# A two-layer encoder in float32: the opening on unscaled tokens, and memory's heads later in layer A

## The chip, the cores and the metric

The kernel runs on one core of one Trainium2 chip, as one program. The metric is the device time in microseconds (us) of one execution; lower is better. The engines have these names: PE is the matrix engine, with its weight loads listed apart as PEld; DVE the vector engine; ACT the scalar (activation) engine; POOL is GpSimd; SP and ACT issue the DMAs here.

## The reference

One sequence of 1024 tokens of width 1024, and 256 memory tokens of the same width, go through two layers, A and B. All data is float32.

```
h = RMSNorm(x)
[q_tok | k_tok | v_tok | q_mem] = h @ W_in
y_tok = windowed grouped attention (layer A)  or  2-D neighbourhood attention (layer B)
y_mem = softmax(q_mem k_mem^T) v_mem      # 4 heads; k_mem, v_mem = RMSNorm(mem) @ W_mem of that layer
x = x + concat(y_tok, y_mem) @ W_out
x = x + SwiGLU(RMSNorm(x))
# at the end one more RMSNorm
```

Layer A has 12 query heads and 4 key and value heads of width 64, a window of 128 tokens to each side, a slope by distance and a sink logit per head. RMSNorm multiplies each token by one number (the inverse root of its mean square) and each of the 1024 features by a gain.

## The kernel before

*Layout and precision.* Activations lie transposed: features on the 128 partitions, in 8 pieces of 128 features (index k), tokens in the free dimension, in two halves of 512 (index f). A float32 product is made of three matmuls: each operand is split into a high part (`hi`, a cast on ACT) and the rest (`lo`, a subtraction on DVE), and high x high, high x low and low x high are added in PSUM (`three`, `steps`). A "unit" is 128 output columns of a projection; for one half of the tokens it takes 8 steps of 3 matmuls over 512 columns.

*Opening.* It runs before layer A's attention, in the block with the pool `mp`. Memory comes first: memory's tokens times their gain are split without the RMSNorm number (`mhl`), so that PE can begin before any sum of squares is known. Eight memory units follow, four of each layer (two of keys, two of values), each 24 matmuls over the 256 memory tokens. A key unit's result is multiplied by the RMSNorm number and split. A value unit's result must have tokens on the partitions: it is copied, transposed by PE (`mvT`, L366), then scaled per partition and split (`finish_wm`). Between them the RMSNorm of x goes on: `Norm.add` squares pieces, `sums` adds and averages them with small matmuls (`st`) and takes the power on POOL, `scale` broadcasts the result over the partitions by a matmul (`bc`), and `split` makes the scaled, split tokens `hT` (one multiplication on DVE, `hi`, `lo` for each piece and half). Then `first_dense` computes the first half of the tokens for three units of layer A, `FIRST[0] = [0, 10, 8]`: the first query and key (qk 0), the first memory queries (qm 0) and the first values (v 0). `first_units` in the layer does their second halves. Memory's keys and values are stored to DRAM and loaded again by the layer.

*Layer A's attention.* A list of heads is worked through in halves of 512 queries (32 halves). For each half there are scores (PE, then DVE for bias and maximum, ACT for the exponential), a scaling on POOL, transposes of the probabilities (`turn`) and the product with the values (`mix`). Between these, `pull` takes steps of the other projection units, in the order `names`, at a rate that meets each unit's due time. Unit results are put from PSUM into queries, keys and values by `put`. Finished pairs of heads go to DRAM (`y_d`), and are loaded and split again for the output projection (`load_y`, `out_units`), in the order `pairs`. The mixer of the channels follows, and layer B with the same structure; neither is touched except for `load_stored`.

*Buffers around the change.* PSUM has eight banks: two "mm", two "S", three "T", one "O". Weights `whl` have three buffers. The order of the instructions on each engine is fixed when the kernel is built: the planner takes them by program order as it believes them to be ready, so an instruction can stand ahead of one written before it.

## Time and profile before

| | |
|---|---|
| median of 3 runs | 2135.7 us (2135.16 to 2138.38) |
| span of the profiled execution | 2130.8 us |
| time of that execution beside its span | not given; the span is 4.9 us below the median |
| PE busy | 2097.1 us, 98% |
| DVE, ACT, POOL busy | 71%, 50%, 27% |
| granted PE clock, mean | 0.998 |

A row of a timeline reads: start, duration, engine, line, operation, output <- inputs, shapes, count, and in brackets how long the engine had been idle and what ended that. Matmuls are pipelined: the duration of a row is longer than the distance to the next start. In views by line, a group has its busy time, the mean time of one instruction in ns, then the idle time before it.

### The profile page before, as it was taken

Reading aid. Unit: us, or ns where it says so; the run is one execution under the profiler, and the core shown is the slowest. Engines: PE = TensorE matmul, PEld = TensorE weight load, DVE = VectorE, ACT = ScalarE, POOL = GpSimd, SP = SyncE. Lnnn points to the kernel's source line nnn. Section 1 sums busy time; section 2 is a strip of 40 time slices with the busy share of each in tenths; the row PEclk is TensorE's granted clock in tenths of the full one; section 3 lists DMA queues with packets and bytes.
Section 4 is the critical chain, followed back from the end, with each engine's and each line's share of the span. In section 5 each row is a group of like instructions: output and inputs, shape, how many; then the busy total and the mean of one; then the engine's idle time right before and its main releaser. Section 6 shows DMA issues by size and latency. Waiting matters only on the chain.

```text
span 2130.8 us, 29089 instructions
## 1 busy us (share of the span) xinstructions
PE 2097.1 (98%) x10320; PEld 1752.8 (82%) x10320; DVE 1517.2 (71%) x2481; ACT 1065.8 (50%) x2046; POOL 576.8 (27%) x618
## 2 busy tenths in 40 slices
PE   8999999999999999999999999999999999999998
PEld 7788888878888888888778888888888888888887
DVE  7677787788666666867766666667976666677676
ACT  6577775443434334344465666654443434344442
POOL 0343330233443430000233223203243443410000
PEclk9999999999999999999999999999999999999999
DMA  6321028323323327866232222275233323267662
GB/s 247 114 92 44 31 68 295 112 90 123 109 90 111 105 106 252 307 210 210 70 92 82 73 62 68 87 254 165 64 113 112 109 95 114 100 246 258 199 226 89
DMA packets 121042, 287.29 MB, mean 135 GB/s; under 512 B 12224, under 2 KB 20672, under 8 KB 120896
## 3 DMA queue, kind: packets, MB, share of 16 engines
q1 hardware_dynamic: 113584, 272.71, 38.1%
q10 hardware_dynamic: 7312, 12.72, 1.6%
q8 instruction: 82, 1.34, 0.3%
q14 instruction: 64, 0.52, 0.1%
HBM read 210.40 MB, written 68.94 MB: 131 GB/s over the span
## 4 chain that ended last, share of the span: by engine, by line
PE 90%; DVE 3%; ACT 3%; DMA 1%; issue 1%; POOL 1%; SPq 0%; DVEq 0%; ACTq 0%; POOLq 0%
PE X L952 17%; PE Y L952 16%; PE mm L139 16%; PE X L1383 11%; PE Y L1383 8%; PE po L139 8%; PE S L619 3%; PE O L682 3%; PE pT L662 3%; PE X L1034 2%; PE Y L1034 2%; DMA wd_kept<-in_w_dn 1%; POOL wS L909 0%; DMA x<-in_x 0%; PE bc L255 0%
## 5 line engine op out<-in xcount | busy, mean ns | idle before, releaser
L952 PE MATMUL Y<-hB,wgu 128*128 128x512 f32 x1056 | 255.5, 391 | 0.8 <-ACT c L972 0.8
L952 PE MATMUL X<-hB,wgu 128*128 128x512 f32 x1056 | 254.8, 391 | 0.0
L1383 PE MATMUL X<-hB,wd 128*128 128x512 f32 (+1 forms) x1092 | 243.8, 383 | 1.0 <-DVE x L1347 1.0
L109 DVE TENSOR_TENSOR wgu<-wS,wgu 128x1024 fp32r<-128x1024 f32 (+1 forms) x124 | 152.9, 1233 | 121.8 <-ACT wgu L106 121.5
L1383 PEld LDWEIGHTS X<-hB,wd 128*128 128x128 f32 x1092 | 200.1, 188 | 42.0 <-issue 2.4
L952 PEld LDWEIGHTS Y<-hB,wgu 128*128 128x128 f32 x1056 | 196.7, 188 | 43.4 <-ACT c L972 1.7
L952 PEld LDWEIGHTS X<-hB,wgu 128*128 128x128 f32 x1056 | 195.9, 188 | 39.9
L647 POOL TENSOR_SCALAR p<-p,stat 128x384 f32<-128x384 f32 (+1 forms) x256 | 139.7, 565 | 310.8 <-DVE stat L644 207.5
L139 PE MATMUL mm<-hT,wqk 128*128 128x512 f32 x672 | 196.1, 405 | 1.5 <-DVE KL L109 1.5
L106 ACT CAST wgu<-wS 128x1024 fp32r<-128x1024 f32 (+1 forms) x124 | 114.3, 923 | 149.6 <-POOL wS L909 124.6
L139 PE MATMUL po<-yT,wo 128*128 128x512 f32 x768 | 184.8, 394 | 0.0
L1383 PE MATMUL Y<-hB,wd 128*128 128x512 f32 x792 | 180.7, 389 | 0.1
L1383 PEld LDWEIGHTS Y<-hB,wd 128*128 128x128 f32 x792 | 148.5, 188 | 31.6 <-ACT hB L106 0.5
L240 POOL TENSOR_TENSOR nr<-nv,neg_half 128x4 f32<-128x4 f32 (+1 forms) x12 | 11.3, 938 | 600.5 <-DVE nv L239 600.5
L139 PEld LDWEIGHTS po<-yT,wo 128*128 128x128 f32 x768 | 142.8, 188 | 29.7 <-issue 1.0
L952 PE MATMUL X<-hT,wgu 128*128 128x512 f32 x624 | 150.2, 391 | 0.0
L106 ACT CAST hB<-b_raw 128x512 fp32r<-128x512 f32 x154 | 89.5, 618 | 110.6 <-DMA b_raw<-b_d 95.0
L909 POOL TENSOR_TENSOR wS<-wgu_raw 128x512 f32<-128x512 f32 x44 | 61.1, 1388 | 294.8 <-DVE wgu L109 294.8
L952 PEld LDWEIGHTS X<-hT,wgu 128*128 128x128 f32 x624 | 116.8, 188 | 26.3
L634 ACT ACTIVATE p<-p,stat 128x256 f32<-128x256 f32 (+1 forms) x192 | 112.4, 587 | 51.5 <-DVE stat L630 49.2
L109 DVE TENSOR_TENSOR pl<-pT,ph 128x384 fp32r<-128x384 f32 (+1 forms) x256 | 118.0, 493 | 19.4 <-ACT ph L106 16.5
L952 PE MATMUL Y<-hT,wgu 128*128 128x512 f32 x528 | 129.9, 390 | 0.0
(185 smaller groups left out, 4201.5 us busy)
## 6 DMA issues: line engine op xcount, KB each, us to landing
wgu_raw<-in_w_gu SPq DMA_DIRECT2D x92, 512.0 KB
wd_raw<-in_w_dn SPq DMA_DIRECT2D x70, 512.0 KB
b_raw<-b_d SPq DMA_DIRECT2D x70, 512.0 KB
b_d<-c SPq DMA_DIRECT2D x88, 256.0 KB
b_d<-t SPq DMA_DIRECT2D x66, 256.0 KB
wo_raw<-in_w_out SPq DMA_DIRECT2D x32, 512.0 KB
xr_d<-x ACTq DMA_DIRECT2D x32, 256.0 KB
xr<-xr_d SPq DMA_DIRECT2D x16, 512.0 KB
```

What stands on the lines that cost most here:

```text
L106: nc.scalar.copy(dst, src)
L109: (eng or nc.vector).tensor_tensor(dst, src, h.bitcast(F32), op=ALU.subtract)
L139: nc.tensor.matmul(ps[:, :n], l, r, start=start and i == 0 and j == 0, stop=stop and i == len(order) - 1 and j == 2,)
L619: nc.tensor.matmul(s_[:, :n], Q[self.h][:, qb * P : (qb + 1) * P], k, start=j == 0, stop=j == 1)
L634: nc.scalar.activation(p[:, :n], p[:, :n], AF.Exp, bias=m1, scale=-1.0, accum_out=s1)
L647: nc.gpsimd.tensor_scalar(p[:, :n], p[:, :n], ri[:, i : i + 1], 1.0, op0=ALU.mult, op1=ALU.mult)
L662: nc.tensor.transpose(tr[:, j * P : (j + 1) * P], p[:, j * P : (j + 1) * P], ident)
L682: nc.tensor.matmul(o[:, c0 : c0 + w * P], self.value(j), t[:, s0 : s0 + w].rearrange("p j q -> p (j q)"), start=j == js[0] and t is self.p ...
L909: sub = lambda o, p_, q_: nc.gpsimd.tensor_tensor(o, p_, q_, op=ALU.subtract)
L952: nc.tensor.matmul(ps, l, r, start=n in (0, 1, 3, 6) and k == 0 and i == 0, stop=k == 3 and i == 2, skip_group_check=True,)
L1034: nc.tensor.matmul(bank[:, at : at + h2], l, r, start=start and k == 0 and i == 0, stop=stop and k == 1 and i == 2, skip_group_check=True,)
L1383: nc.tensor.matmul(bank[:, c], l, r, start=i in (0, 1, 3, 6) and p == 0 and n == 0, stop=p == HF - 1 and n == 2, skip_group_check=True,)
```

## The change

Layer A's projections are no longer made from scaled tokens. The tokens are multiplied by the gain and split (`unscaled`: one operation on ACT, one on DVE for each piece), without waiting for the RMSNorm number; the number, broadcast over the partitions, is kept as `unit_scale`, and every result of a projection unit of layer A is multiplied by it when read from PSUM (DVE).

The opening now begins with x: two units (qk 0 and v 0) on both halves of the tokens, four runs of 24 matmuls, into four PSUM banks. They are read, scaled, when the norms are known (`scaled_sums`, `first_sums`), and put into place by `ready_units` at the start of the layer. Memory's units come after, in the order values, keys of layer A, values, keys of layer B. A value unit is computed with memory's tokens as the stationary operand, so its result has tokens on the partitions and needs no transpose: 48 matmuls over 128 columns in place of 24 over 256. Memory's results wait in the three "T" banks. Sums of squares are taken on pieces of 1024 columns (`total`), and the mean and broadcast use the one "O" bank. The pieces of x share seven buffers, so the eighth is loaded when the first is free.

In layer A the memory queries (qm 0) are no longer in the opening but one of ten units pulled between attention work; the heads of memory come after heads 0 to 5 and after heads 6 to 9, and 16 steps are pulled around `ready_units` and one more with each step of the first scores. `load_stored` loads finished pairs only.

```diff
-FIRST = [0, 10, 8], [0, 18, 12]
+FIRST = [0, 8], [0, 18, 12]
...
+        raws = [raw_tile("wf_raw") for _ in range(2)]
+        src = [a["w_in_a"][u] for u in FIRST[0]]
+        nc.scalar.dma_start(raws[0][:, :HS], src[0][:, :HS])
+        load_x(0, 0, each=True)
+        nc.scalar.dma_start(gains, a["gains"])
         load_x(0, 2)
+        nc.scalar.dma_start(raws[0][:, HS:], src[0][:, HS:])
         load_x(0, 4)
         load_x(0, 6)
+        nc.sync.dma_start(raws[1], src[1])
+        load_x(1, 0)
+        load_x(1, 2)
+        load_x(1, 4)
+        nc.sync.dma_start(memt[:, :4], a["mem"][:, :4])
+        load_x(1, 6)
+        nc.sync.dma_start(memt[:, 4:], a["mem"][:, 4:])
+        load_wm(0)
...
+        def unscaled(f, k):
+            g = gains[:, 0, k : k + 1]
+            t = hp.tile([P, 2, HS], F32R, tag="h", name="hT")
+            nc.scalar.activation(t[:, 0], x[k][f], AF.Copy, scale=g)
+            nc.vector.scalar_tensor_tensor(
+                t[:, 1], x[k][f], g, t[:, 0].bitcast(F32), op0=ALU.mult, op1=ALU.subtract
+            )
+            hT[f][k] = t
...
+        split_raw(wf[0], raws[0], cs=slice(0, HS))
+        for k in range(4):
+            unscaled(0, k)
+        split_raw(wf[0], raws[0], cs=slice(HS, D))
+        for k in range(4, NK):
+            unscaled(0, k)
+        parts = total(norms[0], [xp[k, 0] for k in range(0, NK, 2)])
+        run_some(parts, 1)
+        sums = [ps_mm.tile([P, HS], F32, tag="mm", name="mm") for _ in range(2)]
+        sums += [ps_s.tile([P, HS], F32, tag="S", name="mm") for _ in range(2)]
+        run(steps(sums[0], wf[0], hT[0]))
+        split_raw(wf[1], raws[1])
+        for k in range(NK):
+            unscaled(1, k)
+        run(steps(sums[1], wf[1], hT[0]))
+        run(steps(sums[2], wf[0], hT[1]))
...
+        run(steps(sums[3], wf[1], hT[1]))
...
+        def mem_dense(i):
+
+            w, ps = whl[i], ps_t.tile([P, HS], F32, tag="T", name="mm")
+            mem_sums[i] = ps
+            if mem_order[i][1] < 2:
+                run(steps(ps, w, mh, n=NM))
+                return
+            for b in range(2):
+                c = slice(b * P, (b + 1) * P)
+                for k in range(NK):
+                    for n, (l, r) in enumerate(three(wk(w, k), (mh[k][:, 0, c], mh[k][:, 1, c]))):
+                        nc.tensor.matmul(
+                            ps[:, c], r, l, start=b == 0 and k == 0 and n == 0,
+                            stop=k == NK - 1 and n == 2, skip_group_check=True,
+                        )
...
+        def scaled_sums(f):
+
+            nc.scalar.copy(unit_scale[f], norms[f].scale())
+            for n in range(2):
+                nc.vector.tensor_tensor(first_sums[n][f], sums[2 * f + n], unit_scale[f], op=ALU.mult)
...
             if i == 1:
+                scaled_sums(0)
+                mem_norm.sums()
+                parts = total(norms[1], [xp[k, 1] for k in range(0, NK, 2)])
+                run_some(parts, 2)
             if i == 2:
+                nc.scalar.copy(scale, mem_norm.scale())
+                run(parts)
                 nc.vector.tensor_scalar(nsink, sink, -1.0, None, op0=ALU.mult)
+            if i == 4:
+                norms[1].sums()
+            if i == 5:
+                scaled_sums(1)
+            if i > 1:
+                finish_wm(i - 2)
             if i > 5:
+                early.append(load_w(a["w_in_a"][(1, 2)[i - 6]], name="wf"))
...
                 def half(self, f, bank=None):
                     ps = bank.tile([P, HS], F32, tag="T", name="mm") if bank else mm_tile()
                     yield from steps(ps, self.w, hT[f])
+                    if is_a and self.kind == "v":
+                        nc.vector.tensor_tensor(placed(self.vt, f), seen(ps), seen(unit_scale[f]), op=ALU.mult)
+                        return
+                    if is_a:
+                        t = temp("u")
+                        nc.vector.tensor_tensor(t, ps, unit_scale[f], op=ALU.mult)
+                        ps = t
                     self.put(f, ps)
...
+            if is_a:
+                heads = [*range(6), ("m", 0), ("m", 1), *range(6, 10), ("m", 2), ("m", 3), 10, 11]
+                pairs = [0, 1, 2, 6, 3, 4, 7, 5]
...
+                names = [("qk", 0), ("v", 0), ("qq", 0), ("qk", 1), ("qq", 1), ("qm", 0),
+                         ("qk", 2), ("v", 1), ("qq", 2), ("qk", 3), ("qm", 1), ("qq", 3)]
...
+            if is_a:
+                biases[heads[0]] = make_bias(heads[0])
+                ready_units()
+                for _ in range(NK):
+                    pull()
+            for _ in halves[0].scores():
+                if is_a:
+                    pull()
```

## The prediction

> **What bounds the kernel now.** I read the page first: how busy each engine is, the granted clock, the chain that ended last.

> ```profile
> span 2130.8 us, 29089 instructions
> PE 2097.1 (98%) x10320; PEld 1752.8 (82%) x10320; DVE 1517.2 (71%) x2481; ACT 1065.8 (50%) x2046; POOL 576.8 (27%) x618
> PE 90%; DVE 3%; ACT 3%; DMA 1%; issue 1%; POOL 1%; SPq 0%; DVEq 0%; ACTq 0%; POOLq 0%
> ```

> PE carries 90% of the chain; what does not shorten PE's work or fill a gap in it changes nothing. The span is 4.9 us below the median of 2135.7 us; the page gives no other time for that execution, so I work in differences and put them on the median. The edit lies in the opening and in layer A's attention, so next come the busy times by stretch (columns: PE, weight loads, DVE, ACT, POOL, PE's clock, DMA).

> ```profile
> 0.00:46.30 46.30, 37.32 (x226) 32.05 (x226) 34.70 (x64) 31.15 (x56) 1.92 (x6) 0.96 0.71 261
> 46.30:81.20 34.90, 34.86 (x158) 28.51 (x159) 26.24 (x44) 16.41 (x32) 3.54 (x3) 1.00 0.49 158
> ...
> 100.00:220.00 120.00, 117.57 (x669) 99.25 (x668) 87.44 (x236) 90.20 (x242) 50.10 (x90) 1.00 0.20 65
> 220.00:322.00 102.00, 99.88 (x575) 83.93 (x574) 82.92 (x222) 79.77 (x216) 35.72 (x64) 1.00 0.17 55
> ```

> Only the first 46 us have PE visibly idle. A pipelined matmul's busy time flatters, so I go by distances between starts, in PE's timeline of the opening:

> ```profile
> 5.84 9.11 PE L139 MATMUL mm<-mhl,wm 128*128 128x256 f32 x48 [1.44 <-ACT mhl L339]
> 18.54 3.09 PE L139 MATMUL mm<-mhl,wm 128*128 128x256 f32 x24
> 21.47 1.02 PE L255 MATMUL bc<-diag,ones 128*128 128x512 f32 x2
> 21.92 3.41 PE L139 MATMUL mm<-mhl,wm 128*128 128x256 f32 x24
> 29.16 1.22 PE L255 MATMUL bc<-diag,ones 128*128 128x256 f32 x2 [1.84 <-DVE diag L243]
> 46.34 6.65 PE L139 MATMUL mm<-hT,wf 128*128 128x512 f32 x28 [2.50 <-DVE wf L109]
> 55.37 0.95 PE L219 MATMUL st<-inv_d,sq 128*128 128x1 f32 x8
> 59.02 22.15 PE L139 MATMUL mm<-hT,wf 128*128 128x512 f32 x95
> 81.00 0.28 PE L619 MATMUL S<-mKH,QS 128*128 128x256 f32 x1
> ```

> A 512-column matmul takes 21.98/95 = 0.231 us (59.02 to 81.00), so 24 of them (half a projection unit) take 5.55 us and a unit 11.1 us. A memory unit of 24 matmuls over 256 columns takes 2.93 us (18.54 to 21.47). By 81.0 us PE has done eight memory units (23.4 us) and three projection units (33.3); with mean and broadcast matmuls some 62 us are work and 19 us are not. The losses: 5.84 us before the first matmul, waits for x and for the first sums, and DVE twice late (before 29.16 and 46.34). That is all the opening can give, under 1% of the time.

> **The change, part by part.** The mark for comparison: PE has finished all memory units and two projection units. The kernel before is there at 81.0 - 11.1 = 69.9 us, its third unit taken off; after the change that unit (qm 0) is pulled later between attention work, at the same 11.1 us.

> *Start.* The first work becomes half a unit on unscaled x. Its operands need x from memory and one ACT and one DVE operation per 128 rows:

> ```profile
> 12.18 1.15 ACT L203 ACTIVATE sq<-x 128x512 f32<-128x512 f32 x2 [0.21 <-DMA x<-in_x]
> 14.88 1.15 ACT L203 ACTIVATE sq<-x 128x512 f32<-128x512 f32 x2 [0.19 <-DMA x<-in_x]
> 4.75 0.62 ACT L106 CAST wm<-wm 128x512 fp32r<-128x512 f32 x1 [1.99 <-DMA wm<-in_w_mem]
> 26.58 1.22 DVE L109 TENSOR_TENSOR wm<-wm 128x1024 fp32r<-128x1024 f32 x1
> 59.62 2.06 DVE L276 SCALAR_TENSOR_TENSOR h<-x,gains,bc 128x512 f32<-128x512 f32 x3
> ```

> Two 512 KB pieces of x became usable between 12.18 and 14.88, so one takes 1.35 us and the last had 4.2 MB issued up to it. In the new order the last piece of the first half of x has 2.6 MB, hence about 10.8 us; the second weight follows at 12.1. Two rows of x then need ACT at 0.6 and DVE at 0.7 each, so the last operand is there near 12.9 and PE ends this half at 13.4 (started 5.9, 5.55 of work: 2.0 lost). The second unit's low part is ready at 12.1 + 1.0 (ACT) + 1.2 (DVE) = 14.3; its first third-matmul waits, 0.5 lost, end at 19.4. The second half of x (last piece 18.9, operand 20.9) is ahead of need: 25.0 and 30.5 for the other two halves. On SP's queue the last piece of x waits for a buffer that the first Square frees (about 1.0 us on ACT, from 6 to 13 us); memory's second half, its weights, ident and sink stand behind it. The transfers issued before last to about 17 us, so the queue does not run dry: nothing lost; were that Square 6 us later, a few us of memory's units would be.

> *Memory's values untransposed.* Four of eight units change from 24 matmuls of 256 columns to 48 of 128 columns, each with its own weight load. Rows for so short a matmul:

> ```profile
> 290.77 0.22 PE L682 MATMUL O<-ph,V 128*128 128x128 f32 x1
> 290.83 0.28 PE L682 MATMUL O<-pl,V 128*128 128x128 f32 x1
> 290.95 0.33 PE L682 MATMUL O<-ph,V 128*128 128x256 f32 x1
> 291.12 0.28 PE L682 MATMUL O<-pl,V 128*128 128x256 f32 x1
> ...
> 309.81 1.06 PE L662 MATMUL pT<-ident,p 128*128 128x128 f32 x8
> 310.63 0.42 PE L619 MATMUL S<-KH,QS 128*128 128x384 f32 x1
> ```

> One alone costs 0.06 us (290.77 to 290.83), a pair 0.18, that is 0.09 each, a chain of eight 0.82 or 0.103 each; and after the pair a 256-column matmul still takes 0.17 (290.95 to 291.12), not 0.12. So a load hides only behind a longer matmul. A unit is a chain of 48, nearest to the chain of eight; I take 0.11, a little more since its loads are of the other type, so 5.3 us (ends: 0.06, 2.9 us; 0.122, the pace of a 256-column matmul, 5.9 us). Four units cost 4 x (5.3 - 2.93) = 9.5 us of PE, against eight transposes (about 0.8 us) removed. This speaks against the change and eats most of what the start wins.

> [...]

> *Memory's stage.* A chain of four steps now leads from memory's squares to its first values:

> ```profile
> 27.72 0.15 DVE L239 TENSOR_SCALAR nv<-st 128x2 f32<-128x2 f32 x1
> 27.95 0.70 POOL L240 TENSOR_TENSOR nr<-nv,neg_half 128x2 f32<-128x2 f32 x1 [7.97 <-DVE nv L239]
> 38.83 0.37 ACT L371 ACTIVATE mv<-mvT,nr 128x128 fp32r<-128x128 f32 x1 [0.59 <-PE mvT L366]
> 40.35 0.35 DVE L372 SCALAR_TENSOR_TENSOR mv<-mvT,nr,mv 128x128 fp32r<-128x128 f32 x1
> ```

> The units hold their sums in the three T banks of PSUM, so the fourth waits until the first is read. A mean takes 0.8 (55.37 row, eight matmuls), a broadcast 0.45 (21.47 to 21.92, where the next begins). From 30.5: value unit 35.8, mean of x 36.6, value unit 41.9, broadcast 42.4, key unit 45.3, mean of memory (0.4) 45.7. Then 0.5 (add, hand-over), 0.7 (POOL), two ACT and two DVE steps overlapped, 1.2: the bank is free at 48.1, a new wait of 2.4 us, with memory's broadcast in it. The other four: key 51.0, value 56.3, mean 57.1, value 62.4, broadcast 62.9, keys 65.8 and 68.8. Against 69.9: -1.1 us. DVE's removed work (16 splits of 0.69) counts nothing, since other engines' time is hidden behind PE from 13 us on.

> *Into attention.* Before:

> ```profile
> 83.51 1.79 PE L139 MATMUL mm<-hT,wqq 128*128 128x512 f32 x5 [0.34 <-ACT wqq L106]
> 85.37 4.49 PE L139 MATMUL mm<-hT,wqq 128*128 128x512 f32 x19
> 89.70 0.28 PE L619 MATMUL S<-mKH,QS 128*128 128x256 f32 x1
> ```

> Between 81.00 and 89.70 PE did 24 projection matmuls (5.55), eight score matmuls of 256 columns (0.98) and eight transposes (0.82): 7.35 of 8.70, so 1.35 lost, ended by weights cast late. Now those weights are split during the last memory units, and 28 steps of 0.69 us are pulled before and around the first scores, 19 us of cover for the first queries, keys and values (eight operations of at most 0.7 us on each of ACT and DVE, 5.6 us, and a copy of K by DMA). I take -1.35; zero if the cover fails.

> *Layer A's loop.* Twenty halves are now scaled by DVE when read; in 18 the work is new, in two it replaces an ACT copy. A 512-column read by DVE from PSUM:

> ```profile
> L109 DVE TENSOR_TENSOR QS<-mm,QS 64x512 fp32r<-64x512 f32 x22 | 15.1, 688 | 1.9 <-ACT QS L106 1.0
> PE pT L662 <- DVE pl L109: 2.2, 6, 0.5
> ```

> (The first row is from the view by line for 82 to 322 us: busy time and mean ns of one; the second from the waits.) 20 x 0.69 = 13.8 us over some 250 us, on a DVE that is 73% to 81% busy there; the extra unit lengthens the stretch by 11.1 us of PE at the same time, so its share rises by two points. PE's waits on DVE in that loop sum to 2.2 us. I take +0.5; ends -1 (a bank is now free after one read) and +4 (these waits nearly tripled). Moving the memory heads later moves five loads of keys and values on SP into the loop, where DMA is 20% busy; their stores to memory (three per layer) are issued earlier than before, with nobody waiting: nothing.

> *Unplaced stalls.* The order of each queue is fixed beforehand and missed twice before (1.84 and 2.50 us in the rows). Three such chains remain, one priced above; I take +1.5, ends 0 and 4.3.

> Sum: -1.1 - 1.35 + 0.5 + 1.5 = -0.45 us on 2135.7, so 2135.3.

> **Rivals.** (1) Faster: the 48 loads of a value unit hide better than in the transposes. At 0.09 a unit takes 4.3 us, four units 4 us less: 2131; at 0.06, 2126. For it: the pair's 0.09; against it: the 0.17 behind the pair and the chain of eight. It decides from 0.09 down. Centre 2129; chance 0.22.

> (2) Slower: the bank wait grows. The first value unit's four reads queue on DVE behind the sums of the second half of x (four additions, 4.1 us) and a weight split (1.2 us); the fourth unit then starts 5 us later, and the later ones meet the same behind the mean of the second half, 2 to 4 us. For it: DVE was late in just such a place, 1.84 and 2.50 us; against it: DVE has idle time from 30 us on to do these ahead. It decides when these waits exceed my 2.4 by 4.8 us in all. By 7 to 9 us: 2143; chance 0.21.

> (3) Slower: DVE becomes late in the loop, 4 to 6 us: 2140; chance 0.07.

> (4) The start gains nothing because x comes later than 10.8 us (its pieces shared with weights on ACT's queue): each 1 us is 1 us. Up to 3 us, inside my own range.

> **How the numbers follow.** A measurement of this kernel tells about 0.2% (4.3 us) from no change. My forecast, 2135.3 with an own range of 2131.5 to 2140, has 0.50. Faster 0.23: rival 1 and a little of the start; slower 0.28: (2) and (3); within 0.2% 0.49. The range goes from 2127, between rival 1's two values, to 2144, just past rival 2.

> **What would show it.** In the changed trace: the first 24 matmuls of 512 columns end near 13.4 and four halves near 30.5; 48-matmul groups of 128 columns take 5.3 us; one PE wait of about 2.4 us before the fourth memory unit; memory done near 69 us; no gap between it and the first scores. Value units near 4 us mean rival 1; a PE wait of over 5 us on DVE or ACT in front of a memory unit, rival 2; PE waits on DVE of over 5 us from 80 to 330 us, rival 3. The prediction is also wrong if a pool's moved address makes the output projection or the channel mixer wait, which I counted as nothing.

## The result: 2154.05 us after 2135.43, slower by 0.84%

| kernel | median | range | runs |
|---|---|---|---|
| before | 2135.43 us | 2134.88 to 2138.38 | 4 |
| after | 2154.05 us | 2153.01 to 2155.49 | 4 |

The ratio is 1.0084 (95% interval 1.0069 to 1.0098): 18.6 us slower, where 2135.3 with a range of 2127 to 2144 was predicted. The spans of the two profiled executions are 2152.3 and 2130.8 us, 21.5 apart; that of before lies lower against its median than that of after (4.6 us against 1.8). Views of single executions below therefore add up to some 3 us more than the medians.

PE's timeline of the changed kernel, at the predicted mark and behind it:

```profile
7.02 24.03 PE L139 MATMUL mm<-hT,wf 128*128 128x512 f32 x96 [2.63 <-ACT hT L358]
30.88 5.47 PE L426 MATMUL mm<-wm,mhl 128*128 128x128 f32 x48
36.19 1.00 PE L212 MATMUL st<-inv_d,sq 128*128 128x1 f32 x8
37.05 10.04 PE L426 MATMUL mm<-wm,mhl 128*128 128x128 f32 x48
46.89 2.02 PE L248 MATMUL bc<-diag,ones 128*128 128x512 f32 x2
...
53.15 0.59 PE L248 MATMUL bc<-diag,ones 128*128 128x256 f32 x2
54.97 1.05 PE L212 MATMUL st<-inv_d,sq 128*128 128x1 f32 x8 [1.23 <-ACT mscale L484]
56.74 4.48 PE L139 MATMUL mm<-mhl,wm 128*128 128x256 f32 x24 [0.72 <-DVE mv L449]
61.02 11.04 PE L426 MATMUL mm<-wm,mhl 128*128 128x128 f32 x96
...
78.52 9.50 PE L139 MATMUL mm<-hT,wf 128*128 128x512 f32 x41
...
88.64 12.75 PE L139 MATMUL mm<-hT,wf 128*128 128x512 f32 x55
101.23 0.46 PE L698 MATMUL S<-KH,QS 128*128 128x256 f32 x2
...
104.79 0.44 PE L698 MATMUL S<-KH,QS 128*128 128x384 f32 x1 [2.81 <-DVE stat L709]
```

Memory (all eight of its units) is done at 78.52 us, 8.6 later than before (69.9). The first value unit takes 5.31 us (30.88 to 36.19), the second, the same 48 matmuls with no wait, 9.84 (37.05 to 46.89). The granted clock says why. Here are stretches of that kernel cut where the clock changes (columns: length, busy PE, weight loads, DVE, ACT, POOL, granted clock, DMA share, GB/s):

```profile
37.55:51.20 13.65, 13.65 (x60) 12.62 (x60) 8.82 (x10) 5.75 (x6) 0.94 (x1) 0.50 0.38 121
51.20:58.03 6.83, 4.87 (x37) 4.39 (x37) 3.24 (x8) 2.47 (x6) 1.71 (x2) 1.00 0.00 0
58.03:61.44 3.41, 3.41 (x19) 3.41 (x17) 1.27 (x5) 0.58 (x2) 0.00 (x0) 0.50 0.38 154
...
105.80:109.23 3.43, 3.24 (x10) 2.87 (x10) 2.06 (x8) 3.43 (x10) 2.20 (x4) 0.50 0.99 290
```

PE ran 17.1 us of the opening at half its clock, which costs 8.5 us, and 3.4 us more at the first scores. PE was busy all through both of the opening's stretches: no busy share and no wait shows them.

The rest is in layer A's attention. The same view from the first scores to the first of the long run of output projection matmuls, before and after, then the changed kernel's waits from 75 to 350 us (total, times, longest):

```profile
81.00:324.75 243.75, 238.45 (x1354) 200.29 (x1353) 183.52 (x489) 185.30 (x501) 98.84 (x174) 1.00 0.21 66
```

```profile
101.23:346.00 244.77, 230.88 (x1303) 191.92 (x1302) 193.72 (x500) 182.57 (x491) 104.19 (x170) 0.99 0.19 62
```

```profile
PE pT L741 <- DVE pl L109: 6.0, 11, 1.3
PE S L698 <- DVE stat L709: 3.5, 3, 2.8
PE pT L741 <- POOL p L726: 2.1, 5, 0.8
```

The stretch is as long as before, though less stands in it: 439 matmuls of 512 columns instead of 482, since 96 (two whole units) now run ahead of the first scores. At 0.2315 us each (95 in 21.98 in the kernel before), 43 fewer are 9.95 us, so the stretch loses 1.0 + 9.95 = 11.0 us more. I call this number the *extra loss* below (length less 0.2315 us for each wide matmul of L139, against the kernel before). It contains 1.7 us for each step at half clock in the stretch, of which the changed kernel has one. From the mark to the channel mixer's first matmul it is 345.2 us against 333.2: 12.0 more. With the 8.6 of the opening that is 20.6 of the 21.5; behind the mixer's start the two kernels differ by under 1 us.

### The profile page after: what moved, and what is told of

Its sections match the earlier page's. It is cut to its first block, busy times and chain, and to the rows that moved or that the text cites. A ratio compares the mean times of both kernels' runs of the same rounds, so it can differ in the third digit from the quotient of the medians.

```text
span 2152.3 us, 29213 instructions
## 1 busy us (share of the span) xinstructions
PE 2113.6 (98%) x10404; PEld 1766.6 (82%) x10404; DVE 1525.2 (71%) x2480; ACT 1067.3 (50%) x2028; POOL 579.1 (27%) x614
## 4 chain that ended last, share of the span: by engine, by line
PE 90%; DVE 4%; ACT 3%; issue 1%; POOL 1%; DMA 1%; DVEq 0%; ACTq 0%; POOLq 0%
PE X L1059 16%; PE Y L1059 16%; PE mm L139 15%; PE X L1490 11%; PE Y L1490 8%; PE po L139 8%; PE O L761 3%; PE S L698 3%; PE pT L741 3%; PE X L1141 2%; PE Y L1141 2%; PE mm L426 1%; ACT p L713 1%; POOL p L726 1%; DVE pl L109 0%
## 5 line engine op out<-in xcount | busy, mean ns | idle before, releaser
L109 DVE TENSOR_TENSOR wgu<-wS,wgu 128x1024 fp32r<-128x1024 f32 (+1 forms) x124 | 152.9, 1233 | 122.0 <-ACT wgu L106 121.7
L1490 PEld LDWEIGHTS X<-hB,wd 128*128 128x128 f32 x1092 | 200.1, 188 | 41.9 <-issue 2.3
L726 POOL TENSOR_SCALAR p<-p,stat 128x384 f32<-128x384 f32 (+1 forms) x256 | 146.1, 589 | 300.8 <-DVE stat L723 202.3
L106 ACT CAST wgu<-wS 128x1024 fp32r<-128x1024 f32 (+1 forms) x124 | 114.2, 923 | 149.4 <-POOL wS L1016 124.5
L139 PE MATMUL po<-yT,wo 128*128 128x512 f32 x768 | 186.1, 394 | 0.0
L139 PE MATMUL mm<-hT,wqk 128*128 128x512 f32 x624 | 182.0, 404 | 1.6 <-DVE KL L109 1.6
L139 PEld LDWEIGHTS po<-yT,wo 128*128 128x128 f32 x768 | 142.5, 188 | 30.2 <-issue 1.0
L106 ACT CAST hB<-b_raw 128x512 fp32r<-128x512 f32 x154 | 89.6, 618 | 116.4 <-DMA b_raw<-b_d 97.8
L109 DVE TENSOR_TENSOR pl<-pT,ph 128x384 fp32r<-128x384 f32 (+1 forms) x256 | 118.0, 491 | 19.4 <-ACT ph L106 16.9
L109 DVE TENSOR_TENSOR hB<-b_raw,hB 128x512 fp32r<-128x512 f32 x154 | 100.0, 686 | 42.6 <-ACT hB L106 42.5
```

Source lines behind the costliest of these rows:

```text
L106: nc.scalar.copy(dst, src)
L109: (eng or nc.vector).tensor_tensor(dst, src, h.bitcast(F32), op=ALU.subtract)
L139: nc.tensor.matmul(ps[:, :n], l, r, start=start and i == 0 and j == 0, stop=stop and i == len(order) - 1 and j == 2,)
L726: nc.gpsimd.tensor_scalar(p[:, :n], p[:, :n], ri[:, i : i + 1], 1.0, op0=ALU.mult, op1=ALU.mult)
L1490: nc.tensor.matmul(bank[:, c], l, r, start=i in (0, 1, 3, 6) and p == 0 and n == 0, stop=p == HF - 1 and n == 2, skip_group_check=True,)
```

## The experiments

Each run is compared with the kernel before on the same chip, whose medians were 2135.3 to 2136.0. "Memory done" is the mark of the prediction, less 0.2315 us for each projection matmul beyond the 96 of the two units that PE had done by then; the extra loss is given where the run is about the attention.

| run | median, us | memory done | extra loss |
|---|---|---|---|
| after | 2154.05 | 78.5 | 11.0 |
| e1_v256 | 2138.99 | 62.0 | 11.4 |
| e1_st_early | 2147.49 | 71.4 | 10.9 |
| e1_alt | 2146.31 | 71.8 | 11.1 |
| e1_kdirect | 2152.64 | 77.9 | 8.7 |
| e2_v256_kdirect | 2143.86 | - | 17.3 |
| e2_memfirst | 2151.19 | - | 10.3 |
| e2_noscale | 2152.91 | - | 4.3 |
| e2_b_heads (from before) | 2145.27 | - | 5.4 |
| e3_clk | 2148.41 | 73.0 | 10.7 |
| e3_v256_memfirst | 2136.05 | 63.1 | 10.1 |
| e3_rescale | 2158.92 | 74.0 | 10.3 |
| e3_rescale_late | 2152.37 | - | 4.3 |
| e4_bias_late | 2146.92 | 77.0 | 5.9 |
| e4_v256_mf_bl | 2129.85 | 62.1 | 3.5 |
| e4_v256_mf_bl_pool | 2131.30 | - | 4.5 |
| e4_b_bl (from before) | 2134.42 | - | -1.3 |
| e5_late_noscale | 2143.26 | - | -1.8 |
| e5_v256_late | 2135.12 | - | 7.4 |

### The clock in the opening

*256 columns.* In `mem_dense`, `if mem_order[i][1] < 2:` becomes `if True:`, and `finish_wm` has the copy and the two transposes again.

> Memory's four value units again as 24 matmuls of 256 columns, with the copy and the two transposes per unit; the rest of the change stays. Theory 1 (the granted clock fell to half in the opening because units of 128-column matmuls, a load for each, stand around the mean matmuls): the clock stays at or above 0.95 from 31 to 62 us, all memory units take 2.9 to 3.1 us, memory and two projection units are done near 62 to 64 us instead of 78.5, and about 15 us come off: near 2139. Rival (the clock falls for another reason, such as PE's wait or the mean matmuls alone): the clock still shows 0.50 for some 10 us, memory is done near 70 us and the time is near 2146. Both leave the attention part as it is (12 us lost there against before), so neither gets to the time of before.

2138.99 us (1.0021 of before, 1.0012 to 1.0030), memory done at 62.0, clock 1.00 up to 89 us: theory 1. The opening alone is 7.9 us better than before, and the attention loses 11.4 as in the change. So what the change does first, x before its norm, is worth 8 us; the untransposed values give them away by the time of their own 48 matmuls and by the clock (the next run tells the two apart).

*The mean elsewhere.*

```diff
             if i == 0:
-                norms[0].sums()
...
+        norms[0].sums()
         run(steps(sums[3], wf[1], hT[1]))
```

> The mean of x's first half (eight one-column matmuls) goes from between the first two value units to ahead of the last four matmuls of the fourth half unit; the two value units then run as 96 matmuls of 128 columns without a break. Theory 1a (it is the mean matmuls next to a value unit that bring the clock down): the clock stays at 1.00 through both value units (5.3 us each, 30.9 to 42), memory is done near 70 to 71 us, and 7 to 8 us come off: near 2146.5. Theory 1b (any value unit started in this place brings it down, or the wait for the sums does): the second 48 still take 8 to 10 us at a clock of 0.50 and the time stays within 2 us of 2154.

2147.49 us, 6.6 less. PE's timeline, and the clock over the same time:

```profile
30.67 0.95 PE L212 MATMUL st<-inv_d,sq 128*128 128x1 f32 x8
31.49 1.17 PE L139 MATMUL mm<-hT,wf 128*128 128x512 f32 x4
32.49 10.83 PE L427 MATMUL mm<-wm,mhl 128*128 128x128 f32 x96
```

```profile
30.00:48.00 18.00, 17.70 (x142) 16.63 (x140) 13.71 (x19) 7.93 (x10) 2.63 (x2) 1.00 0.55 163
```

96 matmuls of 128 columns in a row take 10.67 us (32.49 to 43.16), 0.111 each, at the full clock: the value units alone don't bring it down. Theory 1a. Memory is done at 71.4, so the four value units as 48 matmuls of 128 columns cost 9.4 us more than as 24 of 256 (71.4 - 62.0), as the prediction had it (9.5), and the rest up to 78.5 is the clock's.

*Value and key units in turn.*

```diff
-        mem_order = [(0, 2), (0, 3), (0, 0), (0, 1), (1, 2), (1, 3), (1, 0), (1, 1)]
+        mem_order = [(0, 2), (0, 0), (0, 3), (0, 1), (1, 2), (1, 0), (1, 3), (1, 1)]
```

> Memory's units in turn: value, key, value, key in each half of memory, instead of two value units and two key units. Theory 1a (mean matmuls beside a value unit): the mean still follows the first value unit, but 24 matmuls of 256 columns come next; if the clock's dip follows from the value unit and the mean, it still falls near 37.5 us, but only key units and one value unit lie in it: memory done near 76 us, near 2152. Theory 1c (it takes a second value unit behind the mean): the clock stays up, memory done near 70 us, near 2146. The doubled loads by themselves (5.3 us for 48) stay in both.

2146.31 us: the time of 1c, but not its reason. The first value unit and its mean, with a key unit behind, leave the clock up; then the planner put the next mean four matmuls into the second value unit, and the clock fell behind that (stretches of 3 us of this run):

```profile
42.00:45.00 3.00, 3.00 (x28) 3.00 (x28) 2.87 (x5) 1.50 (x2) 1.18 (x1) 0.96 0.78 273
45.00:48.00 3.00, 3.00 (x16) 3.00 (x16) 2.54 (x5) 0.73 (x2) 0.43 (x1) 0.50 0.06 20
```

The traces of all runs together show where the clock changes. Between 20 and 125 us the times at half clock are whole multiples of 3.41 us, and in one execution they lie on one grid: in the changed kernel they begin at 37.55, 58.03 and 105.80, the later two 6 and 20 steps of 3.41 behind the first. This part of each of the 18 traces that show such a time in it, cut on its own grid, gives the columns that PE streamed in each step, as a share of 2212 columns per us (512 in 0.2315); a matmul's columns are spread from its start to the next start, at most over its own duration. Of 451 steps at full clock, all 23 with a share below 0.30 were followed by a step at half clock, 14 of 17 from 0.30 to 0.40, and none of 411 above. A value unit has 128 columns in 0.111 us, 0.52; with the mean, whose eight matmuls have one column each and take 0.86 us, a step comes to some 0.39 (0.38 in the step ahead of the changed kernel's first fall), not the 0.36 of the next run's expectation. From half clock the limit lies lower: of 63 such steps, 26 of the 27 with a share below 0.33 were followed by another, and only one of the 36 above. At half clock the steps of the second value unit reach 0.26 to 0.27, and the clock stays down until a step has key units in it (0.34).

*Wide matmuls between.* The last nine matmuls of the fourth half unit go behind the mean.

```diff
-        run(steps(sums[3], wf[1], hT[1]))
+        run(steps(sums[3], wf[1], hT[1], order=range(NK - 3), stop=False))
...
                 norms[0].sums()
+                run(steps(sums[3], wf[1], hT[1], order=range(NK - 3, NK), start=False))
```

> The last nine matmuls of 512 columns of the fourth half unit go behind the mean, between the two value units; the same work, only placed elsewhere. Theory 1 as it now stands (the granted clock is set for each stretch of 3.41 us, and falls to half after a stretch in which PE streamed under about 0.4 of what it can; a value unit alone gives 0.51, a value unit and the mean 0.36): with the wide matmuls in that stretch it stays above 0.5, the second value unit takes 5.3 us, the dip from 37 to 51 us is gone, and 5 to 7 us come off: 2147 to 2149 (a dip of one stretch behind the wait for the bank near 57 us may remain, 1.7 us). Rival (what brings the clock down is a value unit that follows a mean within a few us, whatever stands between): the second still takes 8 to 10 us, 2152 to 2155.

```profile
28.68 5.47 PE L426 MATMUL mm<-wm,mhl 128*128 128x128 f32 x48
33.99 1.00 PE L212 MATMUL st<-inv_d,sq 128*128 128x1 f32 x8
34.86 2.32 PE L139 MATMUL mm<-hT,wf 128*128 128x512 f32 x9
37.02 5.47 PE L426 MATMUL mm<-wm,mhl 128*128 128x128 f32 x48
```

2148.41 us, as the shares said: the same work in another place, the second value unit 5.31 us, one step at half clock left behind the wait for the bank (from 51.44 us). Its rival, a value unit that follows a mean whatever stands between, is out. This settles the opening.

### The attention: DVE, the order of heads, and SP's queue

*Keys without the DMA.*

```diff
                 def close(self):
-                    if self.kind == "qk":
+                    if is_a and self.kind == "qk" and self.i == 0:
+                        for f in range(2):
+                            src = seen(first_sums[0][f][HD:P])
+                            kh, kl = (placed(t[:HD], f) for t in K[0])
+                            hi(kh, src)
+                            lo(kl, src, kh)
+                    elif self.kind == "qk":
```

> The first keys' high and low parts are written for the even rows by ACT and DVE directly from the stored sums instead of by a copy through a DMA. The order of PE changes by this: the first scores stand behind 48 projection matmuls after memory instead of 96. Theory 2 (the late first scores, for want of that copy, leave nothing to cover the ramp into the attention): 5 to 7 us between 100 and 120 us come back to 1 to 2 us, near 2149. Rival (PE would wait as long at the earlier scores, for casts and for the queries, so the loss only moves forward): within 1.5 us of 2154. The opening up to 78.5 us is as before this edit in both.

> Both edits together: memory's values as 24 matmuls of 256 columns, and the first keys written directly instead of by a DMA copy; scores stand 43 projection matmuls earlier in PE's order. Theory 2 (the late scores are what costs the ramp): 4 to 6 us below the run with 256 columns alone (2139.0), so 2133 to 2135. Rival (the ramp's loss moves on to the next late weight or query, as it did with 128 columns, where this edit brought 1.4 us): 2137 to 2138.5.

2152.64 us, and 2143.86 with the 256 columns, 4.9 worse than without it and above what theory 2 and its rival said (four steps at half clock, from 97 and from 114 us, are 6.8 us of its loss). In the changed kernel the scores did come 11.5 us earlier (89.76), but only 2.3 us of the extra loss went; PE now waits where the filler ends before the next weights are there:

```profile
112.57 0.73 PE L139 MATMUL mm<-hT,wqq 128*128 128x512 f32 x2 [0.59 <-DVE pl L109]
114.05 2.57 PE L139 MATMUL mm<-hT,wqq 128*128 128x512 f32 x10 [0.69 <-POOL wqq L109]
```

The rival holds for the first run (within 1.5 us of 2154): not K's copy alone, and theory 2 in this form falls.

*Order of heads.* In the changed kernel the lists `heads`, `pairs`, `names` and the two early weights are as before (memory's heads first); and the lists of the change are put into the kernel before, whose first memory queries stay in its opening.

```diff
-                heads = [*range(6), ("m", 0), ("m", 1), *range(6, 10), ("m", 2), ("m", 3), 10, 11]
-                pairs = [0, 1, 2, 6, 3, 4, 7, 5]
+                heads = [("m", 0), ("m", 1), *range(6), ("m", 2), ("m", 3), *range(6, NH)]
+                pairs = [6, 0, 1, 2, 7, 3, 4, 5]
```

> Layer A's heads, pairs and units in the order of the kernel before (memory's two heads first, their queries third); everything else as changed. Theory 3b (the loop's 7 us come from the order of heads and units): losses between 120 us and the output projection fall from 18 to 19 us to 11 to 13, and the time to about 2148. Theory 3a (they come from DVE's scaling of each half unit): still 18 to 19 us lost there, the time within 2 us of 2154, but for the ramp, which may move either way by some 2 us since the first scores are other ones.

> The kernel before with layer A's heads and units in the changed order (memory's heads seventh, eighth, eleventh and twelfth; their first queries stay in the opening; rows of the finished pairs loaded in the order in which they were stored). No scaling, no other edit. Theory 3b: the loop loses 6 to 7 us more, 2141 to 2142. Theory 3a: within 2 us of 2135.4, since the order costs nothing by itself.

2151.19 us (2.9 less, between the theories, extra loss 10.3), and 2145.27: 9.5 more than before and above what either theory said. The order does cost in the kernel before, 5.4 us of extra loss, and its first scores come 4.5 us later (85.50), about 1.7 of that by a step at half clock at 46.7 that the profile of before does not have; in the changed one little of its loss is due to it.

*No scaling in the loop.*

```diff
-                    if is_a:
-                        t = temp("u")
-                        nc.vector.tensor_tensor(t, ps, unit_scale[f], op=ALU.mult)
-                        ps = t
                     self.put(f, ps)
```

> Leaves out the multiplication of layer A's half units by the token scale in the loop (the splits read the sums themselves); the output is then not the reference's. All other instructions and the order of heads stay. Theory 3a (DVE's scaling makes PE wait): PE's waits on DVE and POOL between 120 and 345 us fall from about 10 us to 3 to 4, 6 to 7 us come off, near 2147. Theory 3b (order of heads): at most 2 us, 2152 to 2154.

```profile
101.07:339.82 238.75, 230.47 (x1306) 192.66 (x1305) 180.27 (x483) 180.79 (x493) 96.35 (x170) 0.99 0.21 65
```

```profile
379.34 1.02 PE L212 MATMUL st<-inv_d,sq 128*128 128x1 f32 x8 [1.70 <-DVE sq L219]
380.23 7.35 PE L139 MATMUL po<-yT,wo 128*128 128x512 f32 x24
```

The stretch is 6.0 us shorter and its extra loss falls by 6.7, as theory 3a said; PE's wait for `pl` falls from 6.0 to 3.6, and all its listed waits in the stretch from 13.1 to 7.6. But the time is 2152.91, only 1.1 less, since the output projection gives 3 to 4 us back: waits of 0.65 and 1.70 us, and behind the second a step at half clock, in which 24 matmuls take 7.2 us where the changed kernel needs 5.6. By the time alone this run would have cleared DVE.

*Tokens scaled a second time in the opening.* To get rid of the loop's scaling without leaving it out, the stored tokens are scaled, split and put in place of the unscaled ones between memory's units (256 columns in both; the old order of heads in the first).

```diff
+        def scaled(f):
+            for k in range(NK):
+                h = temp("h")
+                nc.vector.scalar_tensor_tensor(
+                    h, x[k][f], gains[:, 0, k : k + 1], unit_scale[f], op0=ALU.mult, op1=ALU.mult
+                )
+                t = hp.tile([P, 2, HS], F32R, tag="h", name="hT")
+                hi(t[:, 0], h)
+                lo(t[:, 1], h, t[:, 0])
+                hT[f][k] = t
+                yield
```

> Memory's values as 24 matmuls of 256 columns, and layer A's heads and units in the order of the kernel before; DVE still scales each half unit. If the two edits add (2139.0 and -2.9): near 2136. From the first scores to the output projection theory 3a (DVE's scaling) expects it as long as in the changed kernel, 243 to 245 us, though 40 or so wide matmuls fewer stand in it than in the kernel before; theory 3b (order) expects 238 or less.

> As the run with 256 columns and the old order of heads, but tokens are scaled and split a second time during memory's units (16 times an operation of 0.7 us and a split on DVE, a split on ACT, where DVE stood idle), so that no half unit is scaled in the loop. Theory 3a: the stretch from the first scores to the output projection shortens by about 6 us (some 4 of that may be given back in the output projection, as in the run without scaling): 2130 to 2134. Rival (DVE's 22 us of extra work in the opening make memory's units late): memory is done 4 or more us later than near 62 us and the time is 2136 to 2140.

> The same second scaling, with the heads and units in the changed order (memory's heads later). Theory 3a alone: as the run with the old order, within 2 us. Theory 3b (the order costs by itself, 5 us or more, as it did in the kernel before): 4 to 8 us above it.

The first came out as the sum of its two edits, 2136.05, even with before. The other two missed by some 25 and 18 us: 2158.92 and 2152.37. DVE had no 22 us to spare there: of the 30 us from 36 to 66 it was busy for 20.0 with the 256 columns alone and for 25.1 in the first of the two. The longest wait that this brought PE (first of the two runs):

```profile
50.89 5.46 PE L139 MATMUL mm<-mhl,wm 128*128 128x256 f32 x24 [4.54 <-DVE mv L454]
```

Four steps at half clock lie among such waits, from 46.84, 50.25, 53.67 and 60.49 us, and memory is done at 74.0 instead of 63.1. With the changed order the loop still answers: the stretch is 238.78 us, as in the run that left the scaling out (238.75). With the old order it does not show, 244.52 us and an extra loss of 10.3 against 10.1 with the scaling; but four steps at half clock behind its first scores are 6.8 of these 10.3, two are 3.4 of the 10.1, so that 3.5 stands against 6.7 without them.

*What stands on SP.* In the run with 256 columns and the old order (e3_v256_memfirst), SP's queue (issue times) and PE just behind its first scores:

```profile
70.03 7.87 SPq L871 DMA_DIRECT2D bias_d<-in_rpb  x10
78.00 0.55 SPq L636 DMA_DIRECT2D KH<-KH  x1
...
79.23 1.90 SPq L608 DMA_DIRECT2D mKH<-memk_d  x2
...
83.22 0.54 SPq L113 DMA_DIRECT2D wqk_raw<-in_w_in_a  x1
```

```profile
90.78 0.39 PE L703 MATMUL S<-mKH,QS 128*128 128x256 f32 x1 [4.26 <-ACT p L710]
```

The rows `bias_d`, sixteen in all, belong to layer B. In the kernel before they are written behind `first_units()`, and though the planner fits six of them into earlier gaps on SP, ten stand behind the first keys' copies:

```profile
73.39 0.53 SPq L552 DMA_DIRECT2D KH<-KH  x1
...
76.48 8.03 SPq L774 DMA_DIRECT2D bias_d<-in_rpb  x10
```

The change puts the work of `first_units` into `ready_units`, which is called further down, and so all sixteen came to stand first. Moving them takes this:

```diff
             else:
-                for r in range(ROWS):
-                    nc.sync.dma_start(bias_d[...], a["rpb"][...])
+                rpb_rows = store_rpb()    # yields after each row
...
             for i in range(len(halves)):
+                if is_a and i > 1:
+                    next(rpb_rows, None)
```

> The changed kernel with the twelve DMAs of layer B's bias rows issued one by one from the third half head on, instead of at once ahead of the copy of the first keys, the dist table and the next weights on SP. Theory 2b (the ramp is made by what stands ahead on SP): the first scores come behind 53 projection matmuls instead of 96, the loss between 100 and 120 us falls by 3 to 5 us, 2149 to 2151. Rival (as with the direct keys: the loss moves to the first weights that are then late, or to the end of the filler): 2152 to 2154.

> 256 columns, old order of heads, and the bias rows later. In the run without the last edit (2136.05) SP issued ten of those rows from 70.0 to 78.0 us, then the first keys' copies, memory's keys at 79 to 82 and the next weights at 83 to 84; PE had no filler left at its first scores and lost 10 us from 80 to 110, with three stretches at half clock. Theory 2b: memory's keys land 8 us earlier, 17 of the 96 matmuls stay behind the first scores as cover, the dip of the clock is gone or one stretch long, and 5 to 8 us come off: 2128 to 2131, faster than both kernels. Rival (the filler's end is what costs, whenever it comes): within 2 us of 2136.

> As the run before in this list, and one of the two low parts of each half unit of queries and keys in the loop is computed by POOL instead of DVE (0.69 us on DVE each, some 11 us in all; on POOL about 1.5 us each by its 256-column subtractions of 0.74 us). Theory 3a (DVE's share is what lengthens the loop): 3 to 5 us below that run. Rival (POOL, already waited for by the transposes, comes late by as much): within 1.5 us of it, or above.

> Control: the kernel before with the bias rows later and nothing else. There SP issued the keys of memory at 62 us and the copies of the first keys at 73 us ahead of the ten rows, and the ramp lost 1.4 us; so within 1.5 us of 2135.5 by every theory.

On the changed kernel 2146.92 us, 7.1 less; more than expected, since the rows cost 5.1 of extra loss and this execution also had one step at half clock fewer in the opening (memory done at 77.0). The planner still put twelve of the sixteen rows into gaps ahead of the first keys' copy (issued at 81.12 here), so it is the last four, 3.1 us on SP, whose place makes this difference. With 256 columns and the old order 2129.85. SP there, and the clock from 30 to 100 us:

```profile
69.10 0.55 SPq L636 DMA_DIRECT2D KH<-KH  x1
...
72.47 1.32 SPq L608 DMA_DIRECT2D mKH<-memk_d  x2
...
75.85 0.54 SPq L113 DMA_DIRECT2D wqk_raw<-in_w_in_a  x1
```

```profile
30.00:100.00 70.00, 66.05 (x406) 56.08 (x405) 46.25 (x86) 38.12 (x83) 16.15 (x23) 1.00 0.48 152
```

Its ratio to before is 0.9971 (0.9960 to 0.9982): this version beats both. The control is within 1.6 us of before, as every theory said (2134.42, ratio 0.9993, 0.9984 to 1.0002), so moving rows that already stand behind the first keys brings nothing. Giving POOL half of the low parts took 10 us off DVE (195.5 to 185.5 busy) and brought nothing, 2131.30: PE waited less for `pl` (3.3 us instead of 4.9) but more for POOL's `p` (3.2 instead of 2.4), and one step at half clock came at 97 us. Theory 3a is thus right about where the loss comes from, but not in the form that DVE's sum of busy time sets it.

In the changed kernel itself the rows delay K's copy by only 2.4 us (SP issues them until 84.9, `KH` was written by ACT at 82.6). The larger part, it seems, comes from the fixed order (the planner's order follows from the rows, but no run changes the order alone): PE's has all 96 filler matmuls ahead of the scores, ACT's has the next weight's cast behind the first exponentials. The changed kernel's SP and ACT:

```profile
81.81 3.13 SPq L866 DMA_DIRECT2D bias_d<-in_rpb  x4
85.04 0.55 SPq L631 DMA_DIRECT2D KH<-KH  x1
88.53 1.04 SPq L113 DMA_DIRECT2D wqq_raw<-in_w_in_a  x1
```

```profile
105.92 1.03 ACT L106 CAST wqq<-wqq_raw 128x1024 fp32r<-128x1024 f32 x1
```

ACT waited for nothing before that cast. With the rows later it runs at 93.76 us, and the first scores stand behind 53 of the 96.

*Both causes away.*

> The changed kernel with the bias rows later and without the scaling in the loop (left out, so the output is not the reference's). If these two are all of the attention's loss: between the first scores and the output projection, wide matmuls counted off, it loses within 1.5 us of the kernel before (5.9 us more with the scaling, 4.3 more with the rows ahead). If order of heads or the late memory heads cost by themselves: 3 to 5 us more than before remain. The time: 2141 to 2145, since part of it may be given back in the output projection.

> 256 columns and the bias rows later, in the changed order of heads. If the edits add (2139.0 and about -5 to -6 for the rows): 2133 to 2134, and the old order of heads is worth 3 to 4 us on top (the run with all three took 2129.85). If the order of heads no longer matters once the rows are away: 2130 to 2131.

```profile
91.27:334.12 242.85, 237.86 (x1350) 200.18 (x1349) 182.81 (x487) 182.73 (x496) 96.44 (x170) 1.00 0.19 63
```

| extra loss, us | rows first | rows later |
|---|---|---|
| with scaling | 11.0 | 5.9 |
| scaling left out | 4.3 | -1.8 |

The two causes add up and, within the 1 to 2 us by which single executions differ here (the control has -1.3), nothing is left of the attention's loss; the changed order of heads costs nothing there by itself. In the left column one step at half clock behind the first scores, 1.7 us, is part of each number; with the rows later it is gone. The time, 2143.26, is 8 us above before: in this execution memory is done 7.9 us later than before (77.8), and what the attention gains is given back in the output projection as above. With 256 columns, late rows and the changed order it is 2135.12, 5.3 us above the same with the old order, where 3 to 4 were expected; in that run PE waits 7.4 us for `pl`, in the other 4.9. So with the scaling in the loop the order does matter. Why it costs 9.5 us in the kernel before, without any scaling, is not settled.

## Why the prediction was wrong, step by step

- *Start.* Predicted 5.9, half units done at 30.5; measured 7.02 and 30.88. The number was right, in part by luck. The prediction has 2.5 us of waits for operands inside; 1.6 were lost, nearly all before 10.2 us, where seven matmuls take the time of fourteen:

```profile
6.83:10.24 3.41, 3.22 (x7) 2.24 (x8) 2.53 (x4) 2.62 (x6) 0.00 (x0) 1.00 0.99 352
13.66:17.07 3.41, 3.41 (x17) 2.74 (x16) 3.38 (x5) 3.12 (x6) 0.00 (x0) 1.00 1.05 396
```

  The last starts before 10.2 us lie 0.43 us apart, those behind it 0.23. The record of the clock in this trace begins only at 10.24 us, and the view gives 1.00 where it has no record. The kernel before has the same slow start: from 5.84 to 11.51 us it does 24 matmuls of 256 columns, which take 2.93 us later.
- *A value unit is 48 x 0.11 = 5.3 us.* Right at the full clock: 5.31 us, and 10.67 for two in a row, 0.111 us a matmul. The row of eight transposes (0.103 each) was the right neighbour, and rival 1 (better hidden loads, 0.09 a matmul or less) was not the case.
- *Mark 68.8, 1.1 better than before.* Measured 78.5. The failed step is that every term of this sum was a duration at full clock. 17.1 us at half clock are 8.5 us; without them the mark would be at 70.0. The trace of before had the sign of it, the clock of 0.96 in its first 46 us, and I read past it.
- *Bank wait 2.4.* Measured 1.23 + 0.72; with memory's broadcast, which the prediction's term contains and which stands ahead of the first of the two (53.15), some 2.5. Right in size, though the first of the two waits is that of a mean for the "O" bank, which the prediction did not have. Rival 2 (a growing bank wait) was not the case.
- *Into attention, -1.35, "28 steps of cover".* The extra loss there is 5.1 us. I counted the cover and not the order of SP: layer B's bias rows came to stand ahead of the first keys and the next weights, and the fixed order spent the cover ahead of the scores. I put the moved loads on SP at nothing, and named only memory's.
- *Loop, +0.5 (ends -1 and +4).* Measured 6.7 (7.7 with the rows later). 13.8 us of DVE were counted rightly (its busy time in the stretch falls by 13.5 when they are left out), but that DVE is idle for 21% of the stretch is no cover: the operation can stand ahead of `pl` on DVE, and PE waits for that (2.4 of the 5.5 us that its waits there lose without the operation). This was rival 3, with 7 in 100 and its sign, waits for DVE above 5 us, in the trace. Here the mechanism was named and the size of the chance was off.
- *Unplaced stalls, +1.5.* What the fixed order cost was in the two terms above, and larger.

Sum: 8.6 + 5.1 + 6.7 = 20.4, in profiled executions that differ by 21.5.

## What to carry to other kernels

Cost matmuls by columns per time as well as by duration: here a value unit of 48 matmuls of 128 columns and eight of one column behind it brought PE to half its clock for 13.65 us without an idle moment, and nine matmuls of 512 columns put between, the same work in another place, kept the second value unit at 5.31 us in place of 9.84 and took 5.6 us off the time (e3_clk). When a function is called later than before, write down what it now stands behind on every queue; here four DMAs of another layer, 3.1 us on the queue, cost 5 us. And look at a cause in its own stretch: a run's total hid a gain of 6 us that was given back 40 us later.

## What the hardware showed that I had not expected

PE had no idle time ahead of the first fall in the changed kernel: the step before it, 34.14 to 37.55, has PE busy throughout, at a share of 0.38:

```profile
34.14:37.55 3.41, 3.41 (x33) 3.41 (x32) 1.54 (x4) 0.00 (x0) 0.08 (x1) 1.00 0.83 256
```
